# Hybrid trunk step: scan decays loaded two chunks ahead, one exp in place of four, an order held on TensorE, the last scan group kept in SBUF, and new column blocks for the first mixer

## The chip, the cores and the metric

One core of a Trainium2 chip runs the whole step. The metric is device time in microseconds (us). Engines: PE = TensorE (matmuls; PEld = its weight loads), DVE = VectorE, ACT = ScalarE, POOL = GpSimd, SP = SyncE, which issues nearly all transfers.

## What is computed

Two layers run over 1024 prompt tokens and 8 sample tokens (1032 columns). Layer 0 is a Conformer convolution mixer, layer 1 a Mamba-2 mixer; each is followed by a SwiGLU feed-forward part and a gated per-layer embedding. All is fp32. The Mamba mixer's scan, cut to what matters:

```python
# heads in 8 groups (g) of 4 (r); sequence in 8 chunks of q = 128; state n = 128, head dim p = 64
a_cum = jnp.cumsum(a, axis=-1)
seg = a_cum[..., :, None] - a_cum[..., None, :]
Lmat = jnp.exp(jnp.where(causal, seg, -jnp.inf))
CB = jnp.einsum('bcign,bcjgn->bcgij', Cc, Bc)
y_diag = jnp.einsum('bcgrij,bcjgrp->bcigrp', CB[:, :, :, None] * Lmat, xdt)
states = jnp.einsum('bcjgn,bcgrj,bcjgrp->bcgrpn', Bc, decay, xdt)
final, prev = lax.scan(lambda s, inp: (inp[1][..., None, None] * s + inp[0], s), s0, (states, chunk_decay))
y_off = jnp.einsum('bcign,bcgrpn,bcgri->bcigrp', Cc, prev, jnp.exp(a_cum))
# then + d_skip * x, * silu(z), RMS norm over each group's 256 channels, and @ w_out (2048 x 1024)
```

## The kernel before

**Products.** Activations lie feature-major: 128 features on the partitions, 1032 tokens along the free axis. Every fp32 operand is split into a high part (ScalarE copy, line 110) and the rest, the low part (VectorE, line 111). A product is three matmuls, high by high, high by low, low by high (`mm3`, lines 130 to 132); `product` sums these over the 8 feature tiles for one block of columns. The blocks of a row of columns are 388, 386 and 258 wide (`BLK`). A weight slab is 128x1024 (512 KB): `slab` loads it into `wraw` (line 124) and splits it into `whi` and `wlo`, two buffers each.

**Order.** The code is written for a scheduler that simulates the engines in time and orders each engine's instructions, the transfers of SP's queue among them; after that each engine goes through its list strictly in order, held up by semaphores. `later(k, fn)` puts work off until k column blocks have been written down. `behind(ins, x)` adds an edge without a semaphore: the scheduler may not place `ins` ahead of `x`.

**First mixer** (lines 551 to 735). The embedding input and `x` are loaded block by block, and the first layer's products start with the block of 388 columns. Blocks are normalised after the product (`SCALED_LATER`).

**The scan** (lines 1360 to 1390) goes through 8 groups g of 8 chunks cc, 64 in all. Beside each chunk it runs a `step`, one 1024-wide input projection with 3 column blocks (six per group, at cc = 0, 1, 3, 4, 5, 7): B, C and two x tiles of the next group, then the two z tiles. Their results are evicted by ScalarE, convolved on VectorE (line 1024), put through SiLU (line 1026), and four blocks later transposed to token-major on TensorE (`to_tokens`, line 1046) and copied out (line 1047). In the last group `first_half` takes the place of the steps: the first half of the output product over y tiles 0 to 7.

A chunk has two parts. `weights_a`, one chunk ahead, loads the chunk's cumulated decays as `am` (256 KB, line 1096; two buffers), takes their Relu with a bias for each of four heads (line 1100) and four exps (line 1102), and multiplies by the masked C-B product. `chunk` then does the products: C by the old state (`ys<-state`, line 1136), the four diagonal ones (`yd`, line 1140), the new state's (line 1152), and on VectorE the sums, the gate and the new state (lines 1157 and 1160). After four chunks `y_out` transposes the gated rows (line 1175), scales them (line 1178) and stores them to `y_d` in DRAM (line 1180).

**The output product.** `load_y` loads a tile of `y_d` back (line 1243) into a ring of three raw buffers and splits it. Its second half runs after the scan: 16 loads of the residual `r2_d` (line 1361, `ha` and `hb`) are issued one behind the other; then the weights' second half is gone through twice, once for each half of the columns (j = 0, 1), each time loaded and split anew. In the second pass the feed-forward part's operand for j = 0 is prepared on VectorE (`entry.prepare(0)`).

Of the kernel before, what the change touches and what calls it, by code (L numbers as in the profile page):

```python
# [16 lines left out]
P = 128  # L17
D = 1024
KT = D // P
# [8 lines left out]
BLK = ((0, 388), (388, 386), (774, 258))  # L28
BLQ = tuple((T // 4 * b, T // 4) for b in range(4))
# [28 lines left out]
def trunk_kernel(ctx: ExitStack, tc: tile.TileContext, I, O):  # L58
# [11 lines left out]
    r_d = dram.tile([KT, P, T], F32, name="r_d")  # L70
    r2_d = dram.tile([KT, P, T], F32, name="r2_d")
# [43 lines left out]

    def slab(src, n, extra=None, bufs=2):
# [7 lines left out]
        nc.sync.dma_start(out=raw[:, :n], in_=src)  # L124
        split(raw[:, :n], hi[:, :n], lo[:, :n])
        return hi[:, :n], lo[:, :n]

    def mm3(out, wh, wl, xh, xl, start, stop, onto=False):
# [3 lines left out]
        TE.matmul(out, lhsT=wl, rhs=xh, start=False, stop=stop, skip_group_check=onto)  # L132
# [99 lines left out]
    def ple_load(i, pt, stage, blocks=BLK, ks=(0, 1)):  # L232
# [6 lines left out]
    def ple_products(pool, ps, i, pt, tag, halves=(0, 1), w=None):  # L239
        for s in halves:  # L240
            w = w or kview(slab(I["w_proj"][i, s], 1024), 2)
            for mm in range(4):
                m = 4 * s + mm
                stg = pool.tile([P, T], F32, name="pstg", tag=tag, bufs=3 if tag == "v" else 2)
                for o, n in BLK:
# [305 lines left out]
    with tc.tile_pool(name="l0", bufs=2, reuse_waits="tile") as pool:  # L551
# [10 lines left out]
        def ready(b):  # L562
            o, n = BLK[b]
# [9 lines left out]
        with tc.tile_pool(name="ple0", bufs=2, reuse_waits="tile") as pp:  # L573
# [5 lines left out]
            for k in range(2):  # L579
# [3 lines left out]
                ple_load(0, pt, lambda k, o, n: praw[k][:, o:o + n], BLK[:1], (k,))  # L583
            ple_load(0, pt, lambda k, o, n: praw[k][:, o:o + n], BLK[1:])
            nc.sync.dma_start(out=vec, in_=I["vec"])
            load_x(*BLK[0])
            w1 = pw1_weights(0)
            for b in BLK[1:]:
# [3 lines left out]
            squares(*BLK[0])  # L592
            if 0 not in SCALED_LATER:
                norm.finish(*BLK[0])
# [7 lines left out]
        with tc.tile_pool(name="conv", bufs=2, reuse_waits="tile") as cp:  # L602
            def pw1(m, out, w=None):
# [3 lines left out]
                for i, (o, n) in enumerate(BLK):  # L607
# [96 lines left out]
            if 0 in SCALED_LATER:  # L704
                norm.finish(*BLK[0])
            for b in (1, 2):
                squares(*BLK[b])
                if b in SCALED_LATER:
                    ready(b)
                    next(it)  # L710
                    norm.finish(*BLK[b])
                else:
                    next(it)
                    norm.finish(*BLK[b])
# [198 lines left out]
    with tc.tile_pool(name="ps1", bufs=1, space=PSUM, reuse_waits="tile") as ps, \  # L913
# [6 lines left out]
        ac = pool.tile([P, 8, NH], F32, name="ac", bufs=1)  # L920
# [6 lines left out]
        for tag, shape, n in (("bf", [512], 3), ("cf", [512], 3), ("btok", [512], 3), ("ztok", [4, 256], 4),  # L927
                              ("am", [4, P], 2), ("L", [4, P], 2), ("cbm", [P], 2), ("xd", [4, 64], 2),
# [5 lines left out]
        def decays():  # L934
# [10 lines left out]
            wh = pool.tile([P, 4, P], F32R, name="wdh", tag="am").rearrange("p a b -> p (a b)")[:, :256]  # L945
            wl = pool.tile([P, 4, P], F32R, name="wdl", tag="am").rearrange("p a b -> p (a b)")[:, :256]
# [35 lines left out]
            for lhs, dst in ((umask, ea), (lraw, dtd), (ones, cd)):  # L982
# [3 lines left out]
                if dst is ea:  # L986
                    S.activation(out=nac.rearrange("p c h -> p (c h)"), in_=b[:, :256], func=AF.Copy, scale=-1.0)
                    S.activation(out=ac.rearrange("p c h -> p (c h)"), in_=b[:, :256], func=AF.Copy)
# [99 lines left out]

        def weights_a(g, cc):
# [4 lines left out]
            am = pool.tile([P, 4, P], F32, name="am", tag="am", bufs=2)  # L1094
            r0 = cc * NH + 4 * g
            nc.sync.dma_start(out=am.rearrange("p r i -> p (r i)"), in_=ac_d[r0 * P:(r0 + 4) * P].partition_broadcast(P))
            L = pool.tile([P, 4, P], F32, name="L", tag="L")
            for r in range(4):

                S.activation(out=am[:, r], in_=am[:, r], func=AF.Relu, bias=ac[:, cc, 4 * g + r:4 * g + r + 1])  # L1100
            for r in range(4):
                S.activation(out=L[:, r], in_=am[:, r], func=AF.Exp, scale=-1.0)
# [20 lines left out]
        def chunk(g, cc, L, cfc, xd, xdd, xs):  # L1123
# [11 lines left out]
            if state is not None:  # L1135
                TE.matmul(yb[:, :256], lhsT=cfc, rhs=state, start=True, stop=True)
# [34 lines left out]
            def y_out():  # L1171
                for i in range(2):
                    b = bank("tp", 2)
                    for k in range(4):
                        TE.transpose(out=b[:, k * P:(k + 1) * P], in_=ztok[:, k, i * P:(i + 1) * P], identity=ident)
# [63 lines left out]

        def load_y(kt, operand):  # L1240
            yr = new_raw()[:, :T]
            y, samples = phases(yr)
            loads.append(nc.sync.dma_start(out=y, in_=phases(y_d[kt])[0]))
            G.tensor_copy(out=samples, in_=ysm[:, kt])
            split(yr, *operand)

        def w_out(half, m):
            return kview(slab(I["w_out"][half, m], 1024), KT)

        Y = []  # L1250
        loads = []

# [71 lines left out]
        fill = None  # L1324
        ahead = weights_a(0, 0)
        for i in range(8 * NG):
            g, cc = divmod(i, 8)
            cur, ahead = ahead, weights_a(*divmod(i + 1, 8)) if i + 1 < 8 * NG else None
# [5 lines left out]
            if i == 0:  # L1334
                flush()
            if i == 8 * NG - 9:
                fill = first_half()
                next(fill)
            chunk(g, cc, *cur, *scale_x(g, cc))
            if i == 8 * NG - 9:  # L1340
                nc.sync.dma_start(out=O["sconv_p"], in_=ncp)
                nc.sync.dma_start(out=O["sconv_s"], in_=cst)
                sample(NG - 1)
            if cc == 1 and g < NG - 1:
# [8 lines left out]
    with tc.tile_pool(name="ps2", bufs=7, space=PSUM, reuse_waits="tile") as ps:  # L1353
# [4 lines left out]
        x = loads[-1]  # L1358
        for j in range(2):
            for m in range(KT):  # L1360
# [178 lines left out]
```

## Time and profile before

| | |
|---|---|
| time, median of 3 runs | 3060.66 us (3051.75 to 3060.86) |
| the profiled execution's own time | 3061.45 us |
| its span, first to last instruction | 3059.7 us |
| TensorE busy | 2931.6 us (96%), 20613 matmuls |
| VectorE, ScalarE, GpSimd busy | 1936.3, 1457.6, 453.9 us (63%, 48%, 15%) |
| mean granted TensorE clock | 0.981 |
| transfers | 325.93 MB, mean 107 GB/s |

The busy time of matmuls is a model of their ends; a busy TensorE can still run at half clock, which the granted clock shows (1.00 is 2.4 GHz, 0.50 is 1.2 GHz). Layer 0 takes the span up to about 1100 us, the scan lies from 1264 to 2115 us, the output product's second half ends at 2233 us, and the second feed-forward part follows.

### The profile page before, as it was taken

To read this page: it belongs to the slowest core of one execution; us is meant where nothing else is said; L and a number is where in the kernel's file an instruction comes from. 1 tells how busy PE (TensorE), PEld (TensorE's weight loads), DVE (VectorE), ACT (ScalarE), POOL (GpSimd) and SP (SyncE) were. 2 spreads that over 40 slices of the span, in tenths; PEclk is the share of its full clock that TensorE was granted. 3 is DMA by queue.
4 is the path that set the end of the run, shared out by engine and by line. 5 is a ranking of instruction groups with operands and counts; after the bars stand their busy time and mean duration, and the time that the engine had idled before them with its cause. 6 is when DMAs were issued, how large, how long until landed. Compare 5 with 4: busy or idle time off the path is not lost.

```text
span 3059.7 us, 51605 instructions
## 1 busy us (share of the span) xinstructions
PE 2931.6 (96%) x20613; PEld 2887.9 (94%) x20613; DVE 1936.3 (63%) x3206; ACT 1457.6 (48%) x2798; POOL 453.9 (15%) x476
## 2 busy tenths in 40 slices
PE   8998989999999999999999999989989999999997
PEld 8998989999999999898999998988889999999997
DVE  7786795555444478566677667765495555444476
ACT  6226653333321155767777777743353333321164
POOL 0001320000000021132343333421210000000022
PEclk9999999999999999999999999999999999999999
DMA  5336532222252224123334343576522222252222
GB/s 184 79 87 202 169 95 91 79 78 74 83 180 91 73 90 132 58 87 90 94 99 110 97 91 93 136 195 152 174 94 80 73 84 83 71 187 83 66 90 87
DMA packets 198066, 325.93 MB, mean 107 GB/s; under 512 B 50241, under 2 KB 120257, under 8 KB 197825
## 3 DMA queue, kind: packets, MB, share of 16 engines
q1 hardware_dynamic: 195520, 314.17, 34.0%
q10 hardware_dynamic: 2304, 8.46, 0.7%
q8 instruction: 162, 2.65, 0.4%
q14 instruction: 80, 0.65, 0.1%
HBM read 241.59 MB, written 72.58 MB: 103 GB/s over the span
## 4 chain that ended last, share of the span: by engine, by line
PE 73%; ACT 10%; DMA 7%; DVE 7%; issue 2%; SPq 0%; POOL 0%; ACTq 0%; DVEq 0%; POOLq 0%
PE a L130 8%; PE a L132 8%; PE a L131 8%; PE pA L130 5%; PE pA L131 5%; PE pA L132 5%; PE mm L130 5%; PE mm L131 5%; PE mm L132 4%; DMA am<-ac_d 4%; PE pC L130 3%; PE pC L132 3%; PE pC L131 3%; ACT am L1100 1%; PE pB L131 1%
## 5 line engine op out<-in xcount | busy, mean ns | idle before, releaser
L130 PE MATMUL mm<-u,whi 128*128 128x258 f32 (+2 forms) x1600 | 520.8, 327 | 17.7 <-ACT whi L110 8.9
L132 PE MATMUL mm<-u,wlo 128*128 128x258 f32 (+2 forms) x1600 | 514.1, 323 | 1.6 <-DVE wlo L111 1.6
L131 PE MATMUL mm<-u,whi 128*128 128x258 f32 (+2 forms) x1600 | 509.6, 319 | 0.5 <-DVE u L111 0.5
L110 ACT ACTIVATE whi<-wraw 128x1024 fp32r<-128x1024 f32 (+1 forms) x199 | 207.8, 1045 | 386.6 <-PE a L131 234.0
L130 PEld LDWEIGHTS mm<-u,whi 128*128 128x128 f32 x1600 | 305.9, 192 | 23.2 <-ACT whi L110 10.0
L131 PE MATMUL a<-hh,whi 128*128 128x388 f32 (+2 forms) x984 | 314.6, 320 | 0.5 <-DVE hh L111 0.5
L130 PE MATMUL a<-hh,whi 128*128 128x388 f32 (+2 forms) x984 | 310.4, 322 | 4.3 <-ACT hh L110 4.3
L132 PE MATMUL a<-hh,wlo 128*128 128x388 f32 (+2 forms) x984 | 314.2, 320 | 0.0
L131 PEld LDWEIGHTS mm<-u,whi 128*128 128x128 f32 x1600 | 306.9, 192 | 2.3 <-DVE u L111 1.0
L132 PEld LDWEIGHTS mm<-u,wlo 128*128 128x128 f32 x1600 | 305.3, 191 | 3.8 <-DVE wlo L111 2.3
L111 DVE TENSOR_TENSOR wlo<-wraw,whi 128x1024 fp32r<-128x1024 f32 (+1 forms) x199 | 245.9, 1236 | 89.2 <-ACT whi L110 86.4
L203 POOL TENSOR_TENSOR stat<-stat,sq 128x258 f32<-128x258 f32 (+2 forms) x70 | 63.8, 912 | 1452.2 <-ACT sq L202 1449.0
L472 DVE TENSOR_TENSOR h<-a,h 128x388 f32<-128x388 f32 (+2 forms) x288 | 145.7, 513 | 186.3 <-PE a L132 185.3
L130 PE MATMUL a<-u,whi 128*128 128x258 f32 (+2 forms) x648 | 204.9, 319 | 9.0 <-ACT u L110 6.7
L132 PE MATMUL a<-u,wlo 128*128 128x258 f32 (+2 forms) x648 | 200.7, 313 | 2.9 <-DVE wlo L111 2.8
L131 PE MATMUL a<-u,whi 128*128 128x258 f32 (+2 forms) x648 | 202.5, 314 | 0.0
L130 PEld LDWEIGHTS a<-hh,whi 128*128 128x128 f32 x984 | 185.1, 189 | 4.9 <-ACT hh L110 4.9
L131 PEld LDWEIGHTS a<-hh,whi 128*128 128x128 f32 x984 | 185.4, 189 | 1.0 <-DVE hh L111 0.8
L132 PEld LDWEIGHTS a<-hh,wlo 128*128 128x128 f32 x984 | 185.5, 189 | 0.1
L1100 ACT ACTIVATE am<-am,ac 128x128 f32<-128x128 f32 x256 | 82.5, 391 | 145.4 <-DMA am<-ac_d 145.4
L111 DVE TENSOR_TENSOR wal<-sa,wah 128x1024 fp32r<-128x1024 f32 x44 | 54.4, 1237 | 151.4 <-ACT wah L110 151.4
L130 PEld LDWEIGHTS a<-u,whi 128*128 128x128 f32 x648 | 123.5, 191 | 12.4 <-ACT u L110 7.7
(354 smaller groups left out, 8494.6 us busy)
## 6 DMA issues: line engine op xcount, KB each, us to landing
wraw<-in_w_in SPq DMA_DIRECT2D x48, 512.0 KB, 5.2
hid<-hid SPq DMA_DIRECT2D x88, 258.0 KB, 2.4
hraw<-hid SPq DMA_DIRECT2D x44, 516.0 KB, 3.6
wraw<-in_w_gate SPq DMA_DIRECT2D x44, 512.0 KB, 3.3
wraw<-in_w_up SPq DMA_DIRECT2D x44, 512.0 KB, 3.2
wraw<-in_w_pw SPq DMA_DIRECT2D x32, 512.0 KB, 3.6
wraw<-in_w_down SPq DMA_DIRECT2D x32, 512.0 KB, 3.8
am<-ac_d SPq DMA_DIRECT2D x64, 256.0 KB, 3.4
```

Source lines behind the costliest of these rows:

```text
L110: S.activation(out=hi, in_=raw, func=AF.Copy)
L111: eng.tensor_tensor(out=lo, in0=raw, in1=as32(hi), op=ALU.subtract)
L130: TE.matmul(out, lhsT=wh, rhs=xh, start=start, stop=False, skip_group_check=onto)
L131: TE.matmul(out, lhsT=wh, rhs=xl, start=False, stop=False, skip_group_check=onto)
L132: TE.matmul(out, lhsT=wl, rhs=xh, start=False, stop=stop, skip_group_check=onto)
L203: return eng.tensor_tensor(out=self.acc[:, o:o + n], in0=self.acc[:, o:o + n], in1=sq[:, :n], op=ALU.add)
L472: V.tensor_tensor(out=h[m][:, o:o + n], in0=a[:, :n], in1=h[m][:, o:o + n], op=ALU.add)
L1100: S.activation(out=am[:, r], in_=am[:, r], func=AF.Relu, bias=ac[:, cc, 4 * g + r:4 * g + r + 1])
```

## The change

- **Decays.** `fetch_decays(i)` loads chunk i's `am`; it is called for chunks 0 and 1 ahead of the scan and for i + 2 in chunk i; `am` has three buffers. Relu's bias is `nac`, negated in place after its last use, so `ac` goes.
- **Exp.** One exp over 128x512 in place of four over 128x128.
- **Order.** The transposes of `to_tokens` and `y_out` and C by the old state are put `behind` the last matmul of the product traced last.
- **Last group.** For g = 7, `y_out` writes into two SBUF buffers (`kept`: one under the tag of z, one that was the ring's third) in place of `y_d`; y tiles 14 and 15 are split from there. Three loads of y (tiles 0 to 2) are issued one chunk earlier, at chunk 54; the ring has two buffers after that. The last group's sample state update runs after its chunk 1, as for the others.
- **Second half of the output product.** Each residual load stands behind the last `y_d` load and the last weight slab's load, beside the tile that uses it. In the first pass the slabs' low parts are stored to `low_d` in DRAM; in the second pass (`slab_again`) they are loaded from there, and only the high part is computed.
- **First mixer.** Its column blocks, and those of all embedding products, are 258, 388, 386 (`BLK0`).

```diff
+BLK0 = ((0, 258), (258, 388), (646, 386))
...
+    def slab_again(src, low):
+        raw = wp.tile([P, 1024], F32, name="wraw", tag="wraw")
+        hi = wp.tile([P, 1024], F32R, name="whi", tag="whi")
+        lo = wp.tile([P, 1024], F32R, name="wlo", tag="wlo")
+        nc.sync.dma_start(out=raw, in_=src)
+        nc.sync.dma_start(out=as32(lo), in_=low)
+        S.activation(out=hi, in_=raw, func=AF.Copy)
+        return hi, lo
...
-        TE.matmul(out, lhsT=wl, rhs=xh, start=False, stop=stop, skip_group_check=onto)
+        last_product[:] = [TE.matmul(out, lhsT=wl, rhs=xh, start=False, stop=stop, skip_group_check=onto)]
...
+            S.activation(out=nac, in_=nac, func=AF.Copy, scale=-1.0)
...
-                TE.transpose(out=bv[:, c], in_=src[:, c * P:(c + 1) * P], identity=ident)
+                behind(TE.transpose(out=bv[:, c], in_=src[:, c * P:(c + 1) * P], identity=ident), *last_product)
...
+        def fetch_decays(i):
+            if i < 8 * NG:
+                g, cc = divmod(i, 8)
+                am = pool.tile([P, 4, P], F32, name="am", tag="am", bufs=3)
+                r0 = cc * NH + 4 * g
+                nc.sync.dma_start(out=am.rearrange("p r i -> p (r i)"),
+                                  in_=ac_d[r0 * P:(r0 + 4) * P].partition_broadcast(P))
+                ams.append(am)
...
-            for r in range(4):
-                S.activation(out=L[:, r], in_=am[:, r], func=AF.Exp, scale=-1.0)
+            S.activation(out=L, in_=am, func=AF.Exp, scale=-1.0)
...
-                TE.matmul(yb[:, :256], lhsT=cfc, rhs=state, start=True, stop=True)
+                behind(TE.matmul(yb[:, :256], lhsT=cfc, rhs=state, start=True, stop=True), *last_product)
...
+                    if g == NG - 1:
+                        yp = phases(kept[i])[0][:, :, 64 * hf:64 * hf + 64]
...
-                    nc.sync.dma_start(out=phases(y_d[2 * g + i])[0][:, :, 64 * hf:64 * hf + 64], in_=yp)
+                    if g < NG - 1:
+                        nc.sync.dma_start(out=phases(y_d[2 * g + i])[0][:, :, 64 * hf:64 * hf + 64], in_=yp)
...
+            if half:
+                nc.sync.dma_start(out=low_d[m], in_=as32(w[1]))
...
+        fetch_decays(0)
+        fetch_decays(1)
         ahead = weights_a(0, 0)
         for i in range(8 * NG):
             g, cc = divmod(i, 8)
+            fetch_decays(i + 2)
...
+            if i == 8 * NG - 10:
+                for kt in range(3):
+                    fetched[kt] = fetch_y(kt)
             if i == 8 * NG - 9:
+                ring.remove(raw2)
+                kept += [pool.tile([P, T], F32, name="kept", tag="zf", bufs=1), raw2[:, :T]]
...
-        x = loads[-1]
-        for j in range(2):
-            for m in range(KT):
-                x = behind(nc.sync.dma_start(out=entry.h[j][m], in_=r2_d[m, :, HT * j:HT * j + HT]), x)
+        def residual(j, *ms):
+            for m in ms:
+                behind(nc.sync.dma_start(out=entry.h[j][m], in_=r2_d[m, :, HT * j:HT * j + HT]), loads[-1], *last_slab)
...
-                w = w_out(1, m)
+                w = w_out(1, m, j == 1)
+                if j == 0:
+                    residual(0, m)
+                    if m >= 4:
+                        residual(1, 2 * m - 8, 2 * m - 7)
```

## Rows read from the trace of the kernel before

**Rows 1.** The page: busy us, share of the span, instructions; one kind of transfer.

```profile
PE 2931.6 (96%) x20613; PEld 2887.9 (94%) x20613; DVE 1936.3 (63%) x3206; ACT 1457.6 (48%) x2798; POOL 453.9 (15%) x476
...
am<-ac_d SPq DMA_DIRECT2D x64, 256.0 KB, 3.4
```

**Rows 2.** Busy time by stage: stretch, us, engines, PEclk, DMA share, GB/s.

```profile
1264.00:1960.00 696.00, 650.66 (x4167) 635.24 (x4166) 470.39 (x839) 512.84 (x1137) 244.80 (x244) 0.96 0.36 94
2122.00:2160.00 38.00, 25.36 (x178) 23.52 (x177) 12.67 (x18) 11.13 (x16) 5.09 (x7) 0.89 0.89 231
2160.00:2200.00 40.00, 40.00 (x324) 39.89 (x324) 15.25 (x21) 11.10 (x20) 8.68 (x9) 0.97 0.45 146
2200.00:2233.00 33.00, 30.88 (x253) 30.26 (x252) 31.94 (x36) 16.97 (x25) 11.94 (x12) 1.00 0.33 105
```

**Rows 3.** TensorE's waits, 1264 to 1960: total us, times, longest us.

```profile
PE tp L1046 <- ACT bf L1026: 26.9, 8, 4.2
PE ys L1136 <- DVE state L1160: 8.0, 6, 1.5
```

**Rows 4.** Timeline of TensorE in group 1: start us, us, ..., [idle before].

```profile
1447.28 0.70 PE L1136 MATMUL ys<-state,cf 128*128 128x256 f32 x2 [1.51 <-DVE state L1160]
1451.74 1.11 PE L1046 MATMUL tp<-ident,bf 128*128 128x128 f32 x4 [3.76 <-ACT bf L1026]
```

**Rows 5.** ScalarE's waits, 1264 to 1960.

```profile
ACT am L1100 <- DMA am<-ac_d: 123.3, 47, 7.2
```

**Rows 6.** Timeline of ScalarE ahead of that stall of group 1.

```profile
1426.00 1.28 ACT L1100 ACTIVATE am<-am,ac 128x128 f32<-128x128 f32 x4 [7.03 <-DMA am<-ac_d]
...
1447.72 1.28 ACT L1100 ACTIVATE am<-am,ac 128x128 f32<-128x128 f32 x4 [2.35 <-DMA am<-ac_d]
...
1451.06 0.63 ACT L1026 ACTIVATE bf<-bf 128x512 f32<-128x512 f32 x1
```

**Rows 7.** The chain that ended last, around 1418: start us, us, what.

```profile
1417.90 8.02 DMA am<-ac_d
```

**Rows 8.** Busy time in four of the stretches at a low granted clock.

```profile
1349.50:1356.30 6.80, 5.28 (x18) 5.28 (x19) 4.19 (x8) 6.76 (x12) 3.97 (x5) 0.52 0.13 50
...
1946.80:1953.60 6.80, 4.91 (x19) 4.91 (x20) 5.52 (x11) 6.76 (x9) 2.60 (x5) 0.52 0.74 242
...
2134.60:2138.00 3.40, 3.04 (x13) 2.74 (x13) 1.52 (x2) 1.06 (x1) 0.00 (x0) 0.53 0.04 11
2155.10:2161.90 6.80, 3.51 (x14) 3.22 (x15) 2.45 (x2) 2.11 (x2) 0.00 (x0) 0.51 0.57 195
```

**Rows 9.** Groups by form, 1264 to 2070: busy us, mean ns, idle before.

```profile
L111 DVE TENSOR_TENSOR wlo<-wraw,whi 128x1024 fp32r<-128x1024 f32 x49 | 62.1, 1267 | 52.9 <-ACT whi L110 50.4 <-DMA out_ssm_s<-s 2.0
L1102 ACT ACTIVATE L<-am 128x128 f32<-128x128 f32 x248 | 57.3, 300 | 2.0 <-PE yd L1140 1.5
```

**Rows 10.** TensorE's waits, 1960 to 2115.

```profile
PE tp L1046 <- ACT xtok L1047: 6.2, 1, 6.2
```

**Rows 11.** ScalarE's waits, 1960 to 2115.

```profile
ACT am L1100 <- DMA am<-ac_d: 22.1, 7, 4.6
```

**Rows 12.** TensorE's waits, 2115 to 2165.

```profile
PE mm L130 <- ACT whi L110: 8.4, 4, 6.1
PE mm L130 <- ACT u L110: 3.7, 1, 3.7
```

**Rows 13.** Timeline of SP's queue, 2120 to 2160.

```profile
2137.93 3.95 SPq L1361 DMA_DIRECT2D ha<-r_d  x8
2142.28 5.30 SPq L1361 DMA_DIRECT2D hb<-r_d  x8
...
2152.00 1.01 SPq L124 DMA_DIRECT2D wraw<-in_w_out  x2
```

**Rows 14.** TensorE's waits, 2200 to 2256.

```profile
PE mm L132 <- DVE wlo L111: 1.6, 2, 1.3
```

**Rows 15.** Line 124, the weight slabs, 2090 to 2235: time to landing.

```profile
DMA to landing us min/median/max: 3.4/3.7/7.2
```

**Rows 16.** TensorE's waits, 0 to 60.

```profile
PE a L130 <- ACT ph L110: 5.9, 2, 4.7
```

More of the change, by code (lines that the diff above doesn't have):

```diff
@@ L70, in trunk_kernel @@
     r_d = dram.tile([KT, P, T], F32, name="r_d")
+    low_d = [dram.tile([P, 1024], F32, name=f"low{m}") for m in range(KT)]
     r2_d = dram.tile([KT, P, T], F32, name="r2_d")
@@ L123, in slab @@
             lo = extra.tile([P, 1024], F32R, name="xlo", tag="xlo", bufs=bufs)
-        nc.sync.dma_start(out=raw[:, :n], in_=src)
+        last_slab[:] = [nc.sync.dma_start(out=raw[:, :n], in_=src)]
         split(raw[:, :n], hi[:, :n], lo[:, :n])
         return hi[:, :n], lo[:, :n]
+    def slab_again(src, low):
[6 more added lines that the diff above has]
+        return hi, lo
+    last_product = []
     def mm3(out, wh, wl, xh, xl, start, stop, onto=False):
@@ L230, in scaled_split, with ple_load @@
         split(t[:, :n], uh[:, o:o + n], ul[:, o:o + n], eng=eng)
-    def ple_load(i, pt, stage, blocks=BLK, ks=(0, 1)):
+    def ple_load(i, pt, stage, blocks=BLK0, ks=(0, 1)):
         for o, n in blocks:
@@ L244, in ple_products @@
                 stg = pool.tile([P, T], F32, name="pstg", tag=tag, bufs=3 if tag == "v" else 2)
-                for o, n in BLK:
+                for o, n in BLK0:
                     a = ps.tile([P, 512], F32, name="a", tag="mm")
@@ L562, in ready @@
         def ready(b):
-            o, n = BLK[b]
+            o, n = BLK0[b]
             for m in range(KT):
@@ L606, in pw1 @@
                 out.append(v)
-                for i, (o, n) in enumerate(BLK):
+                for i, (o, n) in enumerate(BLK0):
                     a = ps.tile([P, 512], F32, name="a", tag="mm")
@@ L1093, in weights_a @@
             bf, cf = grp[g]["bf"][hf], grp[g]["cf"][hf]
-            am = pool.tile([P, 4, P], F32, name="am", tag="am", bufs=2)
-            r0 = cc * NH + 4 * g
-            nc.sync.dma_start(out=am.rearrange("p r i -> p (r i)"), in_=ac_d[r0 * P:(r0 + 4) * P].partition_broadcast(P))
+            am = ams.pop(0)
             L = pool.tile([P, 4, P], F32, name="L", tag="L")
             for r in range(4):
-                S.activation(out=am[:, r], in_=am[:, r], func=AF.Relu, bias=ac[:, cc, 4 * g + r:4 * g + r + 1])
-            for r in range(4):
-                S.activation(out=L[:, r], in_=am[:, r], func=AF.Exp, scale=-1.0)
+                S.activation(out=am[:, r], in_=am[:, r], func=AF.Relu, bias=nac[:, cc, 4 * g + r:4 * g + r + 1])
+            S.activation(out=L, in_=am, func=AF.Exp, scale=-1.0)
             cb = bank("cb")
@@ L1238, in sample_norm, with fetch_y, w_out @@
             later(4, finish)
-        def load_y(kt, operand):
[L1241 to L1248, printed above, removed]
+        def fetch_y(kt):
+            yr = new_raw()[:, :T] if kt < 14 else kept[kt - 14]
+            y, samples = phases(yr)
+            if kt < 14:
+                loads.append(nc.sync.dma_start(out=y, in_=phases(y_d[kt])[0]))
+            G.tensor_copy(out=samples, in_=ysm[:, kt])
+            return yr
+        fetched = {}
+        def load_y(kt, operand):
+            split(fetched.pop(kt) if kt in fetched else fetch_y(kt), *operand)
+        def w_out(half, m, again=False):
+            if again:
+                return kview(slab_again(I["w_out"][half, m], low_d[m]), KT)
+            w = slab(I["w_out"][half, m], 1024)
+            if half:
+                nc.sync.dma_start(out=low_d[m], in_=as32(w[1]))
+            return kview(w, KT)
         Y = []
         loads = []
+        kept = []
         def fresh(k):
@@ L1342, in trunk_kernel @@
                 nc.sync.dma_start(out=O["sconv_s"], in_=cst)
-                sample(NG - 1)
-            if cc == 1 and g < NG - 1:
+            if cc == 1:
                 sample(g)
@@ L1374, in trunk_kernel @@
                             for w in (w_out(1, 0), w_out(1, 1)) for b in range(2)]
+                    residual(0, 0, 1)
                     products_by_k(outs, KT)
```

33 lines of the change are left out of this document (17 added, 16 removed).

## The prediction

> **What bounds the kernel now.** I read the page's first part, then busy time by stage, then in each stage what TensorE waited for, and only then the engine that was named. TensorE is busy 2931.6 of 3059.7 us, so 128 us of idle time is all that the removal of waits can give back directly [rows 1]. By stage [rows 2]: the scan's groups 0 to 6 (1264 to 1960) have 45.3 us of it (696.0 - 650.7) at a granted clock of 0.96, and the stretch from the scan to the second output half (2122 to 2160) has 12.6 us in 38 at 0.89. These two are where the change works.
>
> In the scan TensorE waits 26.9 us in 8 cases for B's SiLU (line 1026) before it can transpose B, and 8.0 us in 6 cases for the running state [rows 3]. The timeline of one group shows both, 1.51 us and then 3.76 us, one behind the other [rows 4]. ScalarE, which owes that SiLU, does not lack speed: it stood 123.3 us in 47 cases at line 1100, waiting for a decay block `am` to land [rows 5]. For the case above: 7.03 us before 1426.0 and 2.35 us before 1447.7; the SiLU starts at 1451.1, just before TensorE goes on [rows 6]. So it ran late by two waits of 9.4 us together, against 5.3 us that TensorE lost. The block's load was issued at 1417.90, only when a buffer had come free behind the exp before it, and landed 8.02 us later [rows 7].
>
> Each such stall has a second price. In the stretches around them the clock is granted at 0.52, that is, at the 1.2 GHz level nearly throughout; TensorE had stood idle just before or at their start. There are eight such stretches up to 1960 us, the first and the last of the long ones shown [rows 8]; TensorE is busy 34.2 us in them (5.28, 3.56, 4.13, 3.83, 4.26, 4.84, 3.40 and 4.91). At 2.4 GHz that would be about half, so 34.2 x 0.48 = 16.4 us are lost.
>
> **The change part by part.** The sum is made against the profiled execution's 3061.45 us (span 3059.7 and 1.75 around it); the median of the runs, 3060.66, lies 0.8 below, less than I can resolve.
>
> *Decays two chunks ahead.* The load of chunk i+2 takes a third buffer, whose last reader is the exp of chunk i-1, traced two chunks before. A chunk is 696 us / 56 = 12.4 us, so two are some 25 us, three times that landing of 8.02. ScalarE's waits for `am` go nearly whole. On SP the issue moves ahead of weight slabs and state loads; it has nothing to wait for and its own 0.3 us is all they lose. What ScalarE gains is not time by itself; TensorE's 26.9 us behind it is. Bounds: 0 (another engine is late at the same place) to 26.9. I take 18.9: all eight go, since the delay of 9.4 is larger than the 5.3 lost, and each leaves 1 us, as the next to be late is VectorE's state, whose waits are 1.3 us each. Of that state's 8.0 us I take half, 4.0: the vector work ahead of it starts when ScalarE delivers, but the chain product, add, product stays. Clock: two of the eight half-speed stretches stay, so 16.4 x 6/8 = 12.3. Together **35.2 us**.
>
> *One exp of four.* Four exps take 57.3 us / 62 = 0.92 us a chunk [rows 9]; a 128x512 SiLU, the nearest row for one pass of that size, takes 0.63 [rows 6]. So 0.29 us x 64 = 18.6 us leave ScalarE, beside its idle time of 183 us (696.0 - 512.8) in the groups [rows 2]: 0 on the path, at most some 0.3 us before a stalled transpose. The negation of `nac` replaces the copy to `ac`: 0.
>
> *Order held.* The no-sync edges add no semaphore; they forbid the scheduler to put a transpose or a state product ahead of the last product traced before it. At the stalls they bind nothing: by the code B's transposes come after the first of a tile's three products, and they stand behind all three; the state product stands behind a tile as well [rows 4]. They keep the scheduler from using ScalarE's new freedom for a worse order. Queued behind a held instruction are the products that follow it, and behind these their evictions. Value 0; bounds +8 (single early transposes) and -64 (a rival, below).
>
> *Last scan group in SBUF, residual loads.* TensorE waits 6.2 us once before z's transposes, for ScalarE [rows 10], which waited for decay blocks there too, 22.1 us in 7 cases [rows 11]. The reloads of `y_d` feed the same products: three of them now start a chunk earlier, but the ring for the other five falls from three buffers to two, so the last of the eight lands later: I take **4** of the 6.2; bounds 0 to 8 (with some 1.8 of clock). The last sample update moves two chunks on, with its loads and stores on SP and its GpSimd work; that thins this stretch, and GpSimd, busy 245 of 696 us [rows 2], covers it later. After the scan the waits are 3.7 us for the operand reloaded from `y_d` and 8.4 for `whi`, of which one is 6.1 [rows 12]. The first goes: tiles 14 and 15 are no longer written and reloaded. The 6.1 has its cause on SP: 16 residual loads are issued from 2137.9 to 2147.6, and the weight slab queued behind them only at 2152.0 [rows 13]. With each residual behind its slab it goes too; the other 2.3 of `whi` stay, as they wait for buffers. With the clock, (3.04 + 3.51) x 0.48 = 3.1 [rows 8], that is 12.9; I take **12**, since the moved loads share the transfers. What is late next there is tiles 12 and 13, which go through two buffers; they have 12 us of products before them.
>
> *Lows of `w_out` stored and reloaded.* Second pass: VectorE is busy 31.9 of 33 us there [rows 2], TensorE waits 1.6 us for `wlo` [rows 14]; eight splits of 1.27 us [rows 9] leave VectorE. Gain 1.5. The reload must land while TensorE works on the slab between: 48 products of 128x258 at 40.0 us / 324 = 0.123 [rows 2], so 5.9 us. The slabs, of the same size, land in 3.7 us at the median and 7.2 at most [rows 15]. So each of eight costs 0 to 1.3 us, in all 0 to 10; 2 taken, near the median. Neighbours on SP (stores of `h_d`, the next slab) are queued behind the reload's wait. The Trainium skill, page "DMA: Bandwidth & Descriptors", section "Queues, rings and completion order", says that all transfers of SP share one row of rings and are taken in ring order on each DMA engine. By that each reload stands behind the raw slab; if that doubles the landing, 7.4 instead of 3.7, each is 1.5 us late, 12 in all, and the sum would give 3021 (an estimate). The trace bears the sense of it out: the block above took 8.02 us [rows 7] against a median of 3.4 for all 64 [rows 1].
>
> *First mixer 258/388/386.* The first operand is smaller: TensorE's first waits are 5.9 us in two cases [rows 16], of which a third less to load and split may save 1. Against that the first product pair covers 5.9 us (48 x 0.123) instead of half as much again (388 columns to 258) for the second block's preparation. Value 0, bounds +3 and -3.
>
> Sum: 35.2 + 4 + 12 + 1.5 - 2 = 50.7; 3061.45 - 50.7 = **3011 us**.
>
> **The rivals.**
> - *The wait moves.* ScalarE comes in time, but TensorE stalls nearly as long on VectorE, busy 470 of 696 us [rows 2]. For it: the state wait stands right ahead of B's [rows 4]. Against: VectorE itself idles for ScalarE, 50.4 us ahead of the weights' splits alone [rows 9]. A third of the scan's part (12) and most of the tail's (9) remain: 3061.45 - 21 = 3040.
> - *All goes:* 26.9 + 8.0 + 16.4 + 8.0 + 12.9 + 1.5 + some 5 of small waits = 79, so 2982. For it: the waits share one cause. Against: VectorE's order is fixed beforehand.
> - *Slower: the held order becomes the wait.* A state product may no longer go early; if the state is not ready when a tile's last product ends, TensorE stands. Price: 1.3 us (8.0 / 6) at each of 48 chunks with a tile, 64 us with the clock untouched: 3011 + 64 = 3075. It decides from the point where product, add and copy of one chunk take longer than the next tile's 11 us; 6 of 48 do so now. Against: those six follow a late ScalarE.
> - *The reloads are late:* each of the eight lows lands at the 7.2 us that one slab took [rows 15], 1.3 after it is needed: 10.4 in place of 2, so 3019. Against: the median of 3.7 leaves 2.2 to spare.
> - *The hold changes nothing,* as the scheduler would keep that order anyway: no other time than the forecast's.
>
> **How the numbers follow.** The forecast 0.54, with its own range 2994 to 3030; the late reloads 0.06; the moved wait 0.18; all goes 0.14; the held order 0.08. No change means within 0.3% (3051.5 to 3069.8), about what a measurement of this kernel can tell. Faster: 0.54 + 0.06 + 0.14 + 0.14 of the moved wait = 0.88. Same: 0.04 of the moved wait and 0.02 of the held order = 0.06. Slower: 0.06. The range takes in both the full removal and the moved wait, 2982 to 3046; outside lie about 0.14.
>
> **What would show it.** Right: ScalarE's wait for `am` under 15 us; no transposition of B with a wait over 1.5 us; granted clock 0.99 in the groups; a group of 8 chunks at 93 to 96 us instead of 99 (696 / 7); no idle time over 2 us of TensorE between scan and second output half. A step is wrong if B's waits stay though `am` is there (ScalarE was not the cause), if waits for `wlo` appear in the second pass, or if the state's waits multiply. The forecast is wrong in whole if VectorE's or ScalarE's own order makes TensorE stop at new places in the groups.

## The result and the profile after

The changed kernel takes 3042.09 us (median of 5 runs, 3037.89 to 3044.07) against 3058.2 us before in the same comparison: ratio 0.9948, 95% interval 0.9933 to 0.9963, so 16 us faster and not 50. The profiled execution took 3043.36 us (span 3041.6), at a mean granted clock of 0.982.

The stages, from the timelines (us; by the starts of TensorE's first product in the scan, of the first and the last diagonal products, and of VectorE's first and last residual sums; "groups 0 to 6" runs from the first diagonal product of group 0 to that of group 7). The last column is the fastest kernel of the study, e11 below:

| stage | before | after | e11 |
|---|---|---|---|
| start to the scan's first product | 1261.9 | 1254.3 | 1254.3 |
| to group 0 | 53.6 | 53.6 | 52.6 |
| groups 0 to 6 | 691.9 | 688.0 | 645.4 |
| last group | 99.2 | 108.5 | 99.7 |
| to the first residual sum | 34.4 | 27.3 | 27.7 |
| second output half | 95.2 | 88.5 | 87.3 |
| rest | 823.5 | 821.5 | 822.5 |

The groups, where 35 us were forecast, gave 3.9. The last group became 9 us longer. The stages after it and the start of the kernel gave 23 together.

The page of the changed kernel, against [rows 1]: TensorE's busy time is the same, and a decay block lands in 3.6 us at the median, 3.4 before.

```profile
PE 2929.6 (96%) x20613; PEld 2889.2 (95%) x20613; DVE 1937.7 (64%) x3198; ACT 1437.5 (47%) x2606; POOL 443.1 (15%) x476
...
am<-ac_d SPq DMA_DIRECT2D x64, 256.0 KB, 3.6
```

Busy time by stage, against the first of [rows 2] and against [rows 8]: the clock of the groups rose from 0.96 to 0.98 only, and stretches at half clock are still there. The second line is one of them.

```profile
1264.00:1960.00 696.00, 655.82 (x4221) 639.42 (x4221) 490.34 (x854) 498.51 (x984) 248.85 (x253) 0.98 0.37 98
1565.10:1571.90 6.80, 5.37 (x24) 5.37 (x25) 6.02 (x12) 5.75 (x14) 1.13 (x1) 0.52 0.53 104
```

TensorE's waits from 1264 to 1960, against [rows 3]: B's waits fell from 26.9 to 9.7 us, near the 8.0 that the forecast left, and the state's 8.0 are gone, of which it left half. But the transposes of the gated rows (line 1198) now wait 22.3 us, where 1.9 us stood before. Their bank comes free when ScalarE has copied out x's transposes (line 1062), and ScalarE is as late as ever.

```profile
PE tp L1198 <- ACT xtok L1062: 22.3, 6, 3.8
PE tp L1061 <- ACT bf L1041: 9.7, 7, 1.5
PE ys L1175 <- DVE yo L1168: 3.0, 6, 1.5
```

There are six such waits of 3.64 to 3.77 us. In TensorE's timeline this one lies across the start of the stretch at half clock shown above:

```profile
1566.53 1.75 PE L1198 MATMUL tp<-ident,ztok 128*128 128x128 f32 x7 [3.75 <-ACT xtok L1062]
```

ScalarE's waits in the same stretch, against [rows 5]: 123.3 us became 130.8.

```profile
ACT am L1124 <- DMA am<-ac_d: 130.8, 49, 6.5
```

Why a third buffer did not help stands in the timelines of SP and ScalarE for one chunk. SP's issue of the block, three hundredths of a microsecond behind the end of the exp three chunks back:

```profile
1410.17 0.33 SPq L1111 DMA_DIRECT2D am<-ac_d  x1
```

ScalarE's Relus and the exp of that same block:

```profile
1417.34 1.28 ACT L1124 ACTIVATE am<-am,nac 128x128 f32<-128x128 f32 x4 [6.11 <-DMA am<-ac_d]
...
1445.44 0.63 ACT L1125 ACTIVATE L<-am 128x512 f32<-128x512 f32 x1
```

The load is issued earlier, and the Relus stand right behind its landing all the same: ScalarE waits 6.11 us for them and does the exp 28 us later. Over chunks 8 to 51 the mean from the first Relu to the end of the exp is 20.7 us before and 33.1 us after. In both kernels the first Relu of a block starts 3.6 to 3.7 us behind the issue of its load (the median of the same chunks), whenever that is. So the scheduler, as these numbers read, puts a Relu where the block is expected to land. An earlier load moves the Relus forward with it, and each still holds up everything behind it on ScalarE until the data is there.

The last group's extra 9 us have another place. TensorE's only wait over 0.5 us from 1995 to 2105 us:

```profile
2048.07 1.22 PE L1175 MATMUL ys<-xdd,btok 128*128 128x256 f32 x2 [6.67 <-DVE yo L1168]
```

VectorE, then GpSimd, then SP ahead of it:

```profile
2040.87 1.74 DVE L1233 TENSOR_TENSOR s<-s,xb 128x512 f32<-128x512 f32 x1 [8.85 <-POOL xb L1231]
...
2047.60 0.42 DVE L1168 TENSOR_TENSOR yo<-ys,ea 128x256 f32<-128x256 f32 x1
```

```profile
2039.80 1.04 POOL L1231 TENSOR_TENSOR xb<-bcb,xdt 128x512 f32<-128x512 f32 x1 [25.21 <-DMA bcb<-bc_d]
```

```profile
2032.84 0.29 SPq L1221 DMA_DIRECT2D bc_d<-bcs  x1
...
2035.28 0.37 SPq L1224 DMA_DIRECT2D bcb<-bc_d  x1
```

The sample state update now stands in the last group's second chunk. Its rows go through DRAM (`bc_d`); GpSimd waits for them, VectorE stands 8.85 us for GpSimd at the update's sum (line 1233), and `yo`, for which TensorE waits, comes behind that sum on VectorE. Behind the wait TensorE has half clock from 2046.6 to 2053.4 us. ScalarE waits longer, for a decay block that SP issues late, but that block is issued only after TensorE's wait has ended, and TensorE does not wait again for what it holds up:

```profile
2049.98 0.38 SPq L1111 DMA_DIRECT2D am<-ac_d  x1
```

```profile
2055.49 0.99 ACT L1124 ACTIVATE am<-am,nac 128x128 f32<-128x128 f32 x3 [16.09 <-DMA am<-ac_d]
```

After the scan the forecast came true in the main. TensorE's waits from 2115 to 2165, against [rows 12]: 8.4 us for `whi` are 1.9, the operand's 3.7 are gone, and 2.1 for a low part are new.

```profile
PE mm L148 <- DVE wlo L113: 2.1, 1, 2.1
PE mm L146 <- ACT whi L112: 1.9, 2, 1.6
```

SP, against [rows 13]: four residual loads, and a weight slab 6 us behind the first of them instead of 14.

```profile
2128.85 1.74 SPq L1406 DMA_DIRECT2D ha<-r_d  x4
...
2134.72 0.42 SPq L128 DMA_DIRECT2D wraw<-in_w_out  x1
```

In the second pass TensorE never waits for a reloaded low part; the reloads (line 138) land in 3.6 us at the median, where the slabs of [rows 15] took 3.7:

```profile
DMA to landing us min/median/max: 3.2/3.6/4.6
```

TensorE's first waits, against [rows 16], are 5.0 us in place of 5.9, and the longest is the same 4.7:

```profile
PE a L146 <- ACT ph L112: 5.0, 2, 4.7
```

### The profile page after: what moved, and what is told of

It is laid out like the page before. It is cut to its first block, busy times and chain, and to the rows that moved or that the text cites. A ratio compares the mean times of both kernels' runs of the same rounds, so it can differ in the third digit from the quotient of the medians.

```text
span 3041.6 us, 51435 instructions
## 1 busy us (share of the span) xinstructions
PE 2929.6 (96%) x20613; PEld 2889.2 (95%) x20613; DVE 1937.7 (64%) x3198; ACT 1437.5 (47%) x2606; POOL 443.1 (15%) x476
## 3 DMA queue, kind: packets, MB, share of 16 engines
q1 hardware_dynamic: 191584, 320.47, 34.4%
## 4 chain that ended last, share of the span: by engine, by line
PE 76%; ACT 8%; DVE 7%; DMA 5%; issue 3%; POOL 0%; SPq 0%; DVEq 0%; ACTq 0%; POOLq 0%
PE a L146 8%; PE a L148 8%; PE a L147 8%; PE pA L146 6%; PE pA L147 5%; PE pA L148 5%; PE mm L146 5%; PE mm L147 5%; PE mm L148 5%; DMA am<-ac_d 3%; PE pC L146 3%; PE pC L148 3%; PE pC L147 3%; PE cacc L700 1%; PE pB L148 1%
## 5 line engine op out<-in xcount | busy, mean ns | idle before, releaser
L112 ACT ACTIVATE whi<-wraw 128x1024 fp32r<-128x1024 f32 (+1 forms) x191 | 199.7, 1046 | 394.2 <-PE a L147 238.1
L1124 ACT ACTIVATE am<-am,nac 128x128 f32<-128x128 f32 x256 | 84.1, 391 | 160.9 <-DMA am<-ac_d 160.9
```

The lines of the kernel that those rows point to most:

```text
L112: S.activation(out=hi, in_=raw, func=AF.Copy)
```

## The experiments

All times are medians of 4 to 11 runs beside 9 to 15 runs of the kernel before on the same chip (3056.4 to 3058.1). The medians of the kernel before differ by 1.7 us between the chips, so 2 us between experiments on two chips can be the chips' own. "A group" is an eighth of the scan by the measure above; groups 0 to 5 are alike, group 6 shorter.

**e1, the Relus in order.**

```diff
-                S.activation(out=am[:, r], in_=am[:, r], func=AF.Relu, bias=...)
-            S.activation(out=L, in_=am, func=AF.Exp, scale=-1.0)
+                behind(S.activation(out=am[:, r], in_=am[:, r], func=AF.Relu, bias=...), *last_exp)
+            last_exp[:] = [S.activation(out=L, in_=am, func=AF.Exp, scale=-1.0)]
```

> The changed kernel with one edit: the four Relus of a chunk are ordered behind the exp of the chunk before, instead of standing where the load of the decays lands. Theory 1 (the third buffer only let the Relus run further ahead, and ScalarE, in order, waits at each landing as before): ScalarE's waits of the Relus for the decays fall from 160.9 us in 54 to under 25 us, the scan's stretch of groups from 728 us to about 700, the time from 3042 to about 3017 (3008 to 3026). Theory 2 (the loads themselves are late, because three buffers come free too late): the waits stay above 80 us. Theory 3 (another engine's order sets the pace of a group, the waits only filled its slack): the waits go, but the time stays within 6 us of 3042.

3010.92 us, ratio 0.9849 (0.9834 to 0.9865): 31 us below the changed kernel. ScalarE's waits and the groups' busy time in the same stretch:

```profile
ACT am L1125 <- DMA am<-ac_d: 2.3, 1, 2.3
```

```profile
1264.00:1960.00 696.00, 664.38 (x4355) 647.05 (x4356) 495.70 (x887) 515.74 (x1009) 250.45 (x262) 1.00 0.40 103
```

130.8 us of waits are 2.3, the clock is 1.00 on the mean, no stretch at half clock lies in the groups up to 1960 us, and groups 0 to 6 take 660.3 us. Theory 1 holds; theory 3, that ScalarE's waits only filled slack, falls.

**e2, the same edit alone on the kernel before** (two buffers, four exps).

> The kernel before with the same edit alone: two buffers, four exps, every Relu ordered behind the exp of the chunk before. Theory 1: the order and not the buffer count is what matters, so the waits fall from 145.4 us to under 40 us and the time from 3058 to about 3033 (3023 to 3043). Theory 2: with two buffers the load is issued only behind the exp two chunks back, so the waits stay above 80 us and the time within 6 us of 3058. Theory 3: the waits go, the time stays within 6 us of 3058.

3014.41 us, ratio 0.9863 (0.985 to 0.9876): 42 us from one ordering edge, more than forecast. Groups 0 to 6 take 644.2 us. ScalarE's waits from 1264 to 1960:

```profile
ACT am L1102 <- DMA am<-ac_d: 14.3, 8, 2.6
```

So the old buffers were enough (theory 2 falls), and a group is 2.3 us shorter here than in e1, which holds all of the change.

**e3, one buffer more and the loads three chunks ahead.**

```diff
-                              ("am", [4, P], 3), ...
+                              ("am", [4, P], 4), ...
...
-            fetch_decays(i + 2)
+            fetch_decays(i + 3)
```

> The changed kernel with a fourth buffer for the decays and the loads three chunks ahead (one of three residual buffers of the last group is given up for the space); the Relus stay unordered. Theory 1: the Relus only run a further chunk ahead of their exp (about 45 us instead of 33), the waits stay at 120 to 170 us and the time within 6 us of 3042. Theory 2: the loads land in time, the waits fall under 50 us and the time by 15 to 25 us.

3040.56 us, ratio 0.9946 (0.9934 to 0.9959), as the changed kernel. The waits in the groups are 131.7 us, and the mean from Relu to exp is now 45.6 us.

**e4, the first mixer's blocks as before** (`BLK0 = BLK`).

> The changed kernel with the first mixer back at 388/386/258 columns. If the 7.6 us that the stages up to the scan took less in the changed kernel come from the block widths, the time rises by 6 to 9 us, to about 3050, with the scan's start back at about 1272 us. If they came from elsewhere (nothing else of the change stands there), the time stays within 2 us of 3042.

3047.70 us, ratio 0.9967 (0.9955 to 0.998): 5.6 us above the changed kernel. The two ratios' intervals overlap; the traces bear the size out. The scan's first product starts at 1258.2 to 1261.9 us in the four kernels with the old blocks (the kernel before, e2, e4, e8), and at 1253.9 to 1257.3 in the fifteen with the new ones: 4.9 us earlier on the mean.

**e5, e6 and e7, TensorE's holds taken out.** e5 and e6 on e1, with no hold and with the state product alone free; e7 on the changed kernel, with no hold. The edit at the state product (at the transposes it is alike):

```diff
-    behind(TE.matmul(yb[:, :256], lhsT=cfc, rhs=state, start=True, stop=True), *last_product)
+    TE.matmul(yb[:, :256], lhsT=cfc, rhs=state, start=True, stop=True)
```

> The changed kernel with the Relus behind the exp of the chunk before, and all three holds of TensorE's instructions taken out (the two kinds of transposes and the state product). Theory 4 (with ScalarE's waits gone, the holds cost: a group of eight chunks took 95.4 us with the holds and 93.1 us in the old kernel with held Relus and no holds): the groups take 93 us, ScalarE's waits for the decays stay under 25 us, and the time falls from 3011 to about 2995 (2988 to 3001). Rival 5 (the 2.3 us come from the single exp or the third buffer): the groups stay at 95 to 96 us and the time within 5 us of 3011.

> As the run before, but only the state product is free; the transposes stay held. The held kernel showed 7.8 us of TensorE's waits for the state and 6.8 us for yo behind it. If theory 4 holds and the held product is the cause, the groups take 93 to 93.5 us and the time is about 2997; if the held transposes are, the groups stay at 95 to 95.5 us and the time within 5 us of 3011.

> The changed kernel with the three holds taken out and the Relus left as they are, so that the landing of the decays still sets ScalarE's pace. Theory 1 says that ScalarE's waits for the decays stay at 120 to 170 us. The holds took out 25 us of TensorE's waits for B and for the state and brought back 25 us for the transposes of the gated y: as I read it they are worth little here, and the time stays within 6 us of 3042; if they are what won the 4 us of the groups, the time rises to 3048 to 3055.

3011.38 (0.9853, 0.9838 to 0.9869), 3013.35 (0.9856, 0.9843 to 0.987) and 3044.54 us (0.9957, 0.9945 to 0.997). Theory 4 falls: the holds neither cost nor bring anything that can be told, and the 2.3 us a group are not theirs.

**e8, the decays' part alone on the kernel before** (third buffer, loads two ahead, one exp).

> The kernel before with the decays' part alone: three buffers, loads two chunks ahead, one exp of four, one table of signs less. Theory 1: the Relus run one chunk further ahead, ScalarE's waits stay at 130 to 170 us, and the time within 6 us of 3057. The prediction had this part at 35 us of gain, so 3021 if it was right after all and something else in the change took the gain away.

3052.94 us, ratio 0.9985 (0.9976 to 0.9994): 3.8 us of the 35.2, and by the interval 2 to 7. Its transposes of the gated rows wait 23.3 us, and e7, without holds, has 23.8 us of them; so it is this part, not the holds, that moved TensorE's waits there.

**e9 and e10, which half of the decays' part costs once the Relus are in order.** Both are e1 with two buffers; e9 has four exps, e10 one.

> The changed kernel with the Relus behind the exp of the chunk before and the decays as in the kernel before: two buffers, loads one chunk ahead, four exps. Theory 6 (held Relus leave the loads enough time with two buffers, and what made the groups 95.4 us instead of 93.1 is the change's decays part itself): groups at 93 us, ScalarE's waits for the decays about 14 us, and the time 3011 less 2.3 times 7 groups, about 2996 (2990 to 3002). Rival 7 (the 2.3 us come from another part of the change, such as the last group or the kept rows): groups at 95 to 96 us, the time 3008 to 3016.

> As the run before with one exp of four chunks' heads instead of four. If theory 6 holds and the single exp is what costs, the groups take 95 to 96 us and the time is about 3011; if the third buffer is what costs, the groups take 93 us and the time is about 2996.

2997.55 us (0.9801, 0.9788 to 0.9815) and 3011.07 us (0.9849, 0.9835 to 0.9862). The third buffer is worth nothing (e10 against e1), and the single exp costs 13.5 us, though it leaves ScalarE less to do. Where it does so can be seen in one chunk, on VectorE with four exps:

```profile
1561.31 0.43 DVE L1175 TENSOR_TENSOR ztok<-yv,ztok 128x256 f32<-128x256 f32 x1
1561.65 0.41 DVE L1186 TENSOR_TENSOR state<-state,ys 128x256 f32<-128x256 f32 x1
```

and with one:

```profile
1567.28 1.42 DVE L1174 TENSOR_TENSOR ztok<-yv,ztok 128x256 f32<-128x256 f32 x1
1568.62 0.41 DVE L1185 TENSOR_TENSOR state<-state,ys 128x256 f32<-128x256 f32 x1
```

GpSimd's multiply of the decays in that second kernel, released by the exp:

```profile
1567.15 1.27 POOL L1133 TENSOR_TENSOR L<-L,cbm 128x512 f32<-128x512 f32 x1 [0.18 <-ACT L L1127]
```

and TensorE, 1.12 us late for the state:

```profile
1569.09 0.70 PE L1161 MATMUL ys<-state,cf 128*128 128x256 f32 x2 [1.12 <-DVE state L1185]
```

The gate's multiply runs beside GpSimd's and takes 1.42 us in place of 0.43, and the state's sum queues behind it. With four exps GpSimd starts at 1561.48, when the gate's multiply is under way, and that one keeps its 0.43.

**e11 and e12, the sample state update back before the last group:** e11 on e9, e12 on the changed kernel.

```diff
             if i == 8 * NG - 9:
...
+                sample(NG - 1)
-            if cc == 1:
+            if cc == 1 and g < NG - 1:
                 sample(g)
```

> The two-buffer, four-exp kernel with the last group's single-step work traced where the kernel before had it, before that group begins, and no longer at its second chunk. Theory 8 (moved into the last group, its loads and stores of the state stand on SyncE's queue ahead of a load of decays, and held up by VectorE they made that load late, with a gap of TensorE of 6.7 us and half clock behind it): the last group up to the second output half takes 6 to 10 us less than in the run without this edit; about 2988. Rival: the last group's own products set it, within 3 us.

> The changed kernel with that edit alone, Relus unordered. Theory 8: TensorE's wait of 6.67 us for yo in the last group goes, the stretch from the first chunk of the last group to its last falls from 108.5 to about 100 us, and the time from 3042 to about 3034 (3030 to 3038). Rival: within 3 us of 3042.

2991.33 us (0.978, 0.9767 to 0.9794) and 3033.37 us (0.9914, 0.99 to 0.9927): 6.2 and 8.7 us gained; the last group takes 99.7 and 98.8 us. The size that theory 8 gave holds, its mechanism does not. In e9 ScalarE waits for no decay block in the last group, and the moved update costs its 6.2 us all the same: TensorE stands 3.9 us for VectorE, and VectorE for GpSimd's part of the update. In e12 ScalarE still waits 15.6 us for blocks there, and TensorE's wait of 6.67 us is gone. What made the delay is the update's own chain on VectorE; e11 and e12 take out the whole of it, so its links are not told apart. TensorE and VectorE in e9:

```profile
1998.05 1.22 PE L1162 MATMUL ys<-state,cf 128*128 128x256 f32 x2 [3.92 <-DVE state L1186]
```

```profile
1996.15 1.51 DVE L1236 TENSOR_TENSOR s<-s,xb 128x512 f32<-128x512 f32 x1 [6.69 <-POOL xb L1234]
```

e11 is the fastest kernel of the study, 67 us below the kernel before and 51 below the changed one.

**e13, e14 and e15, the tail's parts undone one by one in e11:** low parts split again; residual loads in a chain; the last group's rows through DRAM, with the early loads of y gone too.

> The fastest kernel so far (2991.3 us: Relus behind the exp before, two buffers, four exps, single-step work back) with one part of the change undone: in the second pass over the output weights the low parts are split again by VectorE instead of stored and loaded. The prediction had the reload at about 0.5 us of loss or gain (1.5 off, 2 on): 2989 to 2994. Rival: VectorE's splits in the second pass are what the gaps before the products waited for, and the time rises by 4 to 8 us.

> The same fastest kernel with the residual loads as in the kernel before, all sixteen in a chain ahead of the second pass's weights. The prediction put the waits for the first weights behind them at 8.4 us and the loss of clock with them: the stretch of the second output half from 87.4 us to about 95, the time to about 2999 (2996 to 3002). Rival (the kept rows alone took these waits away): within 2.5 us of 2991.3.

> The same fastest kernel with the last group's gated rows written to DRAM and loaded again, and the first three rows of the first half no longer loaded early, as in the kernel before. The prediction had 4 us for the last group and the larger part of 12 us for the entry into the second output half: from the last group's last chunk to the first residual sum 27.6 us become 33 to 35, the time about 2999 (2995 to 3004). Rival (the loads were hidden, and the gain of this stretch is the residual's): within 2.5 us of 2991.3.

2994.59 (0.9794, 0.9781 to 0.9807), 3000.32 (0.9817, 0.9804 to 0.9831) and 2996.98 us (0.9802, 0.9789 to 0.9816). The parts bring 3.3, 9.0 and 5.7 us; the 3.3 are little more than two chips can tell apart. The idle time that comes back, on TensorE in e14:

```profile
2100.17 0.58 PE L146 MATMUL mm<-u,whi 128*128 128x258 f32 x1 [5.79 <-ACT whi L112]
```

and on SP there, nine microseconds of residual loads and then, 15 us behind the first of them, the slab, as in [rows 13]:

```profile
2077.69 3.95 SPq L1410 DMA_DIRECT2D ha<-r_d  x8
2081.74 4.82 SPq L1410 DMA_DIRECT2D hb<-r_d  x8
...
2092.84 1.27 SPq L128 DMA_DIRECT2D wraw<-in_w_out  x2
```

TensorE in e15, and in e13:

```profile
2081.38 0.89 PE L146 MATMUL mm<-u,whi 128*128 128x258 f32 x4 [3.45 <-ACT u L112]
```

```profile
2160.80 0.39 PE L148 MATMUL mm<-u,wlo 128*128 128x258 f32 x1 [1.33 <-DVE wlo L113]
```

**e16 and e17, the single exp with GpSimd held back.** e16 is e11 with one exp; e17 adds to that a copy that changes no value and delays GpSimd (the next chunk's Relus stand behind it).

```diff
-            last_exp[:] = [S.activation(out=L, in_=am, func=AF.Exp, scale=-1.0)]
+            S.activation(out=L, in_=am, func=AF.Exp, scale=-1.0)
+            last_exp[:] = [S.activation(out=L[:, :2], in_=L[:, :2], func=AF.Copy)]
```

> The fastest kernel (2991.3 us: held Relus, two buffers, four exps, single-step work back) with one exp in place of four: the control for the run after it. Groups of 95.4 us instead of 93.1, VectorE's multiply by the gate at about 820 ns instead of 550, time about 3003 (2999 to 3008). If the two-kernel difference seen earlier was chance of one order, within 4 us of 2991.

> The same one-exp kernel with a useless copy of half of the exp's result onto itself on ScalarE right behind it (0.4 us), so that GpSimd's multiply can start only later; the next Relus stand behind the copy. Theory 9 (GpSimd's multiply, started earlier, runs beside VectorE's multiply by the gate, slows it from 550 to 830 ns, and the state's sum behind it comes late for TensorE): the gate's multiply returns to 550 to 620 ns, the groups to 93 to 94 us, the time to about 2993 although ScalarE does more (2990 to 2998). Rival 10 (the single exp itself or its place in the order costs): the groups stay at 95 us or more, the time at 3003 or above.

3007.51 us (0.9838, 0.9824 to 0.9851) and 3000.23 us (0.9813, 0.9799 to 0.9827). VectorE's multiply by the gate from 1315 to 1860 (count, busy us, mean ns, idle before) in e11, e16 and e17:

```profile
L1175 DVE TENSOR_TENSOR ztok<-yv,ztok 128x256 f32<-128x256 f32 x47 | 26.0, 552 | 0.6
```

```profile
L1174 DVE TENSOR_TENSOR ztok<-yv,ztok 128x256 f32<-128x256 f32 x46 | 37.4, 813 | 0.6
```

```profile
L1175 DVE TENSOR_TENSOR ztok<-yv,ztok 128x256 f32<-128x256 f32 x47 | 26.1, 556 | 0.6
```

Groups 0 to 6 take 645.4, 660.6 and 645.9 us: the useless copy gives the groups back 14.7 of 15.2 us, and TensorE's waits for the state from 1315 to 1860 fall from 6.9 to 1.8 us. Theory 9 holds there. The time recovers only 7.3 of 16.2 us: the stretch from the scan's first product to group 0 is 4.3 us longer than in e16 and that from the last group through the second output half 3.9; why stays open.

## Why the prediction was wrong, step by step

**The step that failed** is "ScalarE's waits for `am` go nearly whole", under *Decays two chunks ahead*. It compared the lead of the load (25 us) with its landing (8) and took the Relus' place on ScalarE as given. They have none of their own: they follow the load's landing. The trace before held the sign: waits in 47 of 56 chunks [rows 5], for an operation that started on average 20.7 us ahead of the end of the exp that needs it. There the reader is too early, rather than the load too late, as e2 then showed. With the waits in place, TensorE's went from B's transposes to those of the gated rows, five of the eight stretches at half clock up to 1960 us remained, at other places, and of the 35.2 us of this term 3.8 came (e8). A stop of TensorE at a new place in the groups, through ScalarE's own order, is the sign that the prediction had named for being wrong in whole. One edge that orders the Relus brings 42 us without any buffer (e2), and by itself shows the term's size: the relief was there, the part of the change that was to bring it did not.

**The rivals.** *The wait moves* fits the total (3040 against 3042) by luck: the waits moved, but to another consumer of the same late ScalarE, not to VectorE, and parts with other causes made up the sum. That the stated range of 2982 to 3046 holds 3042 is owed to this rival alone; the forecast's own range ended at 3030. VectorE became the next limit at the running state, as the forecast had it, in e1 (7.8 us in 8 waits); but that goes with the single exp, for with four exps and ScalarE in time the state's waits up to 1960 us are 1.2 us in e2 and none in e9. *The held order becomes the wait* did not happen. *The reloads are late* did not either.

**One exp of four** was costed at 0 and costs 13.5 to 16.2 us in an ordered kernel (e9 and e10, e11 and e16); in the changed kernel, whose Relus are not ordered, it was not measured by itself. The sum had looked for what its ScalarE time might hide, and not for whom it releases sooner.

**Order held**, 0: right (e5 to e7). The state's 8.0 us went with the decays' part (e8, without holds, shows none), not with the hold.

**The last group and the tail** stood at 4 + 12 + 1.5 - 2 = 15.5 us. Their three parts brought 18.0 (e13 to e15): 9.0 for the residual's order, where the wait, its cause on SP and its clock were read rightly; 5.7 for the rows kept; 3.3 for the low parts, which the sum had at a loss of half a microsecond. These sizes are those in e11. The 4 us were read from the 6.2 us that TensorE waits before z's transposes; in the changed kernel 5.3 us of that wait are still there, so the term was read from a wait that the kept rows do not take away. In the second pass the reloads landed at 3.6 us and at most 4.6, not at 7.4. The Trainium skill ("DMA: Bandwidth & Descriptors", section "Queues, rings and completion order") has transfers of one queue taken in ring order on each DMA engine; the doubled landing that the prediction worked out from it does not agree with this row. The moved sample update, read as relief, cost 6 to 9 us (e11, e12). The prediction counted GpSimd's busy time, and not that VectorE, in order, stands where GpSimd waits for the update's load.

**The first mixer** stood at 0, bounds 3 either way, and brought some 5 us (5.6 in e4, outside the bounds): a term that was mis-sized. The first wait hardly moved (4.7 us again); 5.0 of the 7.6 us by which the traces differ up to the scan lie before the layernorm at 282 to 287 us; where exactly stays open.

Together: 3.8 (decays and exp) + 18.0 + 5.6 - 8.7 (sample update) = 18.7 us against 16 measured, though not all were measured in the same kernel.

## What to carry to other kernels

Ask of a wait for data, on an engine that works in order, how long before its use the waiting instruction stands: where it stands far ahead, another buffer moves it further ahead and the wait stays, while an order that puts it close to its use removes the wait. An operation that gets faster releases its successors sooner, so look at what these will run beside. A step that is moved takes its transfers and its waits along; look at each engine that works in order, at the new place, for what will stand behind them.

## What the runs showed of the hardware

VectorE's 128x256 operations with both inputs in SBUF depend on what GpSimd does. In e16, from 1315 to 1860 us, the 22 of the gate's multiplies that overlap no GpSimd operation take 413 ns on average, the other 24 take 1180. Over all, the gate's multiply takes 454 ns on average in the kernel before, 552 in e11 and 813 in e16, and 1.42 us in the single case above. Those with an input in PSUM do not: the state's sum takes 410 or 411 ns in all of these, `yo` 416 to 420. The Trainium skill ("SBUF — State Buffer", section "Who interferes with whom") says that a VectorE instruction with two SBUF inputs contends with a GpSimd instruction that reads SBUF, and that one with at most one SBUF input, outside the two-port modes, does not; these means agree.

The clock came back with the waits: 0.96 before, 0.98 after, 1.00 in e1 for the same stretch of the scan. In the changed kernel each of the five long stretches at half clock in the groups lies at a wait of line 1198 of 3.6 to 3.8 us; a sixth such wait, 3.72 us before 1864 us, has none. In e9 one such wait is left up to 1960 us, 3.82 us before z's transposes at 1949, and with it the one stretch at half clock.
